# 384-row tiles in four slots, and three engine programs aligned to an instruction block, in a kernel that streams one large input

## The chip, the cores and the metric

The kernel runs on one core of one Trainium2 chip. Its engines are called PE (TensorE), VectorE or DVE, ACT (ScalarE), Pool (GpSimd) and SP (SyncE, which here only issues transfers). The metric is the device time of an execution in microseconds (us), as a median over several executions. Beside it each execution has a *span*, from its first to its last instruction.

## The reference, cut to what matters

```python
B, S, D = 8, 2048, 4096            # x: [B, S, D] float32, w: [D, 1] float32
def reference(x, w):
    proj = (x @ w).squeeze(-1)                      # one dot product for each row of x
    cm = np.maximum.accumulate(proj, axis=1)
    is_record = (proj >= cm).astype(np.float32)
    return np.cumsum(is_record, axis=1).astype(np.float32)
```

x is 268.4 MB and each value is used once; everything after the dot products works on 8 x 2048 numbers.

## The kernel before

The rows are cut into groups: three of 512 rows for each of the 8 batches, one of 384, and 128 last rows that are loaded in small pieces. A tile is one group of one batch. Partition p holds `r` successive rows, so a tile of 512 rows is loaded in 128 runs of 64 KB, one of 384 rows in runs of 48 KB. SP issues all loads of x, in order, on one queue. VectorE takes the first 2816 columns of each row (product and sum in one instruction), Pool multiplies the other 1280, ACT sums them. Pool waits for VectorE's signal `go`, ACT for Pool's products, and SP's next load into a slot for VectorE and ACT.

```python
    RS = (4, 4, 4, 3)                 # rows for each partition in each group
    R = RS[0]; NS = 3                 # three slots of R rows
    NG = len(RS); NL = NG - 1
    ...
        for g in range(NG):
            r = RS[g]
            for t in range(B):
                i = SY.dma_start(
                    out=at(g, t)[:, : r * D],
                    in_=x[B - 1 - t, STARTS[g] : STARTS[g] + r * P, :].rearrange(
                        "(p r) d -> p (r d)", r=r
                    ),
                ).then_inc(xs[t], 16)
                u, n = user_before(g, t)
                if n:
                    i._wait_ge(*(free(u, n)))
                if g == t == 0:
                    A.dma_start(out=w_row, in_=w.rearrange(...)).then_inc(ws, 16)
    ...                               # last 128 rows in pieces; stores of out
        with V.Fori(0, NL):           # the 512-row groups: a loop
            group_scans()
            V.sem_inc(psr, -3)
            group_dots(R)
        group_scans()                 # the 384-row group: once more, unrolled
        V.sem_inc(psr, -3)
        group_dots(RS[-1], NL)
    ...                               # the same loop-and-copy on Pool, ACT and PE
```

Of the kernel before, what the change touches and what calls it, by code (L numbers as in the profile page):

```python
# [20 lines left out]
def kernel(  # L21
# [17 lines left out]
    B, S, D = x.shape  # L39
    WC = 512  # L40
    NW = D // WC
    RS = (4, 4, 4, 3)
    R = RS[0]
    NS = 3
    NG = len(RS)
    NL = NG - 1
    N = R * P
    STARTS = [sum(RS[:g]) * P for g in range(NG)]
    S0 = sum(RS) * P
    assert S0 + P == S  # L50
# [29 lines left out]
    def sb(shape, name, **kw):  # L80
        return pool.tile(shape, FP32, name=name, **kw)
# [5 lines left out]
    w2 = sb([P, W2C], "w2")  # L87
    xall = sb([P, NS * R * D], "xall")
    xbuf = [xall[:, i * R * D : (i + 1) * R * D] for i in range(NS)]
    w_sb = sb([P, PC], "w_sb")  # L90
# [23 lines left out]
    def sem(name):  # L114
        return tc.alloc_semaphore(f"{name}_{next(ns)}")

    xs = [sem("xs") for _ in range(B)]
    fr = [sem("fr") for _ in range(B)]
    xq = [sem("xq") for _ in TILES]
    ws, bw, wc, cs, od, oe, psr, pd, pl, go, sd, pa, con, fo, ms, p7, mg = (  # L120
        sem(n) for n in "ws bw wc cs od oe psr pd pl go sd pa con fo ms p7 mg".split()
    )

    V, A, G, T, SY = nc.vector, nc.scalar, nc.gpsimd, nc.tensor, nc.sync

    def dot(xsl, wsl, dst):
        return V.tensor_tensor_reduce(  # L127
            out=xsl, in0=xsl, in1=wsl, scale=1.0, scalar=0.0,
            op0=ALU.mult, op1=ALU.add, accum_out=dst,
        )  # L130

    def add_up(xsl, dst):
        return A.activation(out=xsl, in_=xsl, func=ACTF.Copy, accum_out=dst)  # L133
# [7 lines left out]
    def scans(cm_, cnt_, src, cm0, cnt0, base=1):  # L141
        low = neg.to_broadcast(list(src.shape))
        V.tensor_tensor_scan(  # L143
            out=cm_, data0=src, data1=low, initial=cm0, op0=ALU.max, op1=ALU.max,
        )._wait_ge(psr, base).then_inc(psr, 1)
        V.tensor_tensor(  # L146
            out=src, in0=src, in1=cm_, op=ALU.is_ge
        )._wait_ge(psr, base + 1).then_inc(psr, 1)
        V.tensor_tensor_scan(  # L149
            out=cnt_, data0=src, data1=low, initial=cnt0, op0=ALU.add, op1=ALU.max,  # L150
        )._wait_ge(psr, base + 2).then_inc(cs, 1)

    def at(g, t):
        return xbuf[(t if g < NL else t + NS - 1) % NS]

    def user_before(g, t):
        if t >= NS:
            return t - NS, g + 1
        if g == NL:
            return B - NS + t, g  # L160
        return max(u for u in range(B) if u % NS == t), g

    def free(u, n):
        return (p7, n) if u == B - 1 else (fr[u], 2 * n)

    with tc.tile_critical(no_gpsimd_drain=True):

        for g in range(NG):
            r = RS[g]
# [11 lines that stand above are left out]
                    A.dma_start(  # L181
                        out=w_row, in_=w.rearrange("(k c) one -> k (c one)", k=NW)
                    ).then_inc(ws, 16)
                if t == 4 and g:
                    SY.dma_start(
                        out=out[:, STARTS[g - 1] : STARTS[g]], in_=cnt
                    )._wait_ge(cs, g + 1).then_inc(od, 16)

        def slot(m):
            if m < NS:  # L190
                return None, xbuf[m][:, RS[-1] * D :]
            u = B - NS if m < 2 * NS else B - NS + 1
            return u, at(NL, u)[:, (m % NS) * D : (m % NS + 1) * D]

        freed = {None}

        for i, (m, c0, c1, _, _) in enumerate(TILES):
            u, xb = slot(m)
            d = SY.dma_start(  # L199
                out=xb[:, c0:c1],  # L200
                in_=x[
                    rows_of(m)[0] : rows_of(m)[0] + H,
                    S0 + rows_of(m)[1] : S0 + rows_of(m)[1] + Q, c0:c1,
                ].rearrange("b i d -> i b d"),
            ).then_inc(xq[i], 16)
            if u not in freed:
                freed.add(u)
                d._wait_ge(*free(u, NG))
            if i == len(TILES) - 4:
                SY.dma_start(  # L210
                    out=out[:, STARTS[-1] : S0], in_=cnt[:, : S0 - STARTS[-1]]
                )._wait_ge(cs, NG + 1).then_inc(oe, 16)
# [42 lines left out]
        def group_scans(r=R):  # L255
            n = r * P
            scans(cm[:, :n], cnt[:, :n], ps[:B, :n], cm[:, N - 1 :], cnt[:, N - 1 :])

        def group_dots(r, g=0):
            for t in range(B):  # L260
                b, xb = B - 1 - t, at(g, t)
                if r == R:
                    V.wait_ge(xs[t], 16).then_inc(go, 1)
                for j in range(r):
                    i = dot(
                        xb[:, j * D : j * D + VC], w_v[:, :VC],
                        sum_v[:, j * B + b : j * B + b + 1],
                    )
                    if j == 0 and r < R:
                        i._wait_ge(xs[t], 16).then_inc(go, 1)  # L270
                    elif j == 1:
                        i.then_inc(xs[t], -16)
                i.then_inc(fr[t], 1)

        with V.Fori(0, NL):
            group_scans()
            V.sem_inc(psr, -3)
            group_dots(R)
        group_scans()
        V.sem_inc(psr, -3)  # L280
        group_dots(RS[-1], NL)

        def group_products(r, g=0):
            for t in range(B):
                for j in range(r):
                    xl = at(g, t)[:, j * D + VC : (j + 1) * D]
                    i = G.tensor_mul(out=xl, in0=xl, in1=w_sb).then_inc(pl, 1)  # L287
                    if j == 0:
                        i._wait_ge(go, 1)
                G.sem_inc(go, -1)  # L290

        G.wait_ge(wc, 3)
        with G.Fori(0, NL):
            group_products(R)
        group_products(RS[-1], NL)

        def group_sums(r, g=0):
            for t in range(B):
                b = B - 1 - t
                for j in range(r):  # L300
                    i = add_up(
                        at(g, t)[:, j * D + VC : (j + 1) * D],
                        sum_p[:, j * B + b : j * B + b + 1],
                    )._wait_ge(pl, j + 1)
                i.then_inc(fr[t], 1)
                A.sem_inc(pl, -r)
            A.wait_ge(pd, 1).then_inc(pd, -1)

        with A.Fori(0, NL):
            group_sums(R)  # L310
        group_sums(RS[-1], NL)

        def group_rows(r):
            T.wait_ge(fr[B - 1], 2).then_inc(p7, 1)
            T.sem_inc(fr[B - 1], -2)
            T.wait_ge(od, 16).then_inc(od, -16)  # L316
            for j in range(r):
                for k, l in enumerate((sum_p, sum_v)):
                    i = T.matmul(  # L319
                        out=ps[:B, j : r * P : r], lhsT=l[:, j * B : (j + 1) * B],  # L320
                        rhs=identity, start=k == 0, stop=k == 1,
                    )
                    if j == r - 1:
                        i.then_inc((pd, psr)[k], 1)

        with T.Fori(0, NL):
            group_rows(R)
        group_rows(RS[-1])


        nv = npool = na = nm = on_a = on_g = 0
# [1 line left out]
        def sums(i, dst_v, dst_p):  # L333
            nonlocal nv, npool, na
            m, _, _, v, p = TILES[i]
            xb = slot(m)[1]
            dot(xb[:, v[0] : v[1]], w_v[:, v[0] : v[1]], dst_v)._wait_ge(
                xq[i], 16
            ).then_inc(sd, 1)
            nv += 1  # L340
            if p:
                xl = xb[:, p[0] : p[1]]
                G.tensor_mul(out=xl, in0=xl, in1=w_pool(*p))._wait_ge(  # L343
                    xq[i], 16
                ).then_inc(pl, 1)
                npool += 1
                add_up(xl, dst_p)._wait_ge(pl, npool).then_inc(pa, 1)
                na += 1
# [90 lines left out]
```

## Time and profile before

| what | value | view |
|---|---|---|
| time, median of 3 (4 with the run beside the changed kernel) | 631.57 (631.58) us | times of the runs |
| span of the profiled execution | 630.02 us | page |
| x queue | 268.50 MB, 98.8% of 16 DMA engines | page, part 3 |
| VectorE busy | 406.9 us (65%) | page, part 1 |
| 512-row tile, landing to landing | 19.35 us (433.5 GB/s) | chain of waits |
| 384-row tile, landing to landing | 14.53 us | chain of waits |
| first x packet starts; last x packet ends | 2.00 us; 624.45 us | packet records of the trace |

The page of the kernel before, its DMA part and one line of the costliest groups (line, engine, operation, operands, count, then busy us and mean ns of one, then idle time before and what ended it):

```profile
DMA  9999999999999999999999999999999999999995
...
DMA packets 6579, 268.55 MB, mean 426 GB/s; under 512 B 768, under 2 KB 1040, under 8 KB 1584
...
q1 hardware_dynamic: 6560, 268.50, 98.8%
...
q14 instruction: 3, 0.02, 0.0%
...
L127 DVE CUSTOM_DVE_ANT_0 xall<-xall,w_v 128x2816 f32<-128x2816 f32 (+3 forms) x133 | 388.4, 2974 | 187.8 <-DMA xall<-in_x_dram 187.8
```

The 16 DMA engines have work in all but the last slice, and VectorE's idle time is all wait for x. The stream is the bound. The line `q14 instruction: 3` is three packets of instructions, of 8,192 bytes each, that were fetched during the span, over the same DMA engines (the one at 126.4 us below starts where an x packet ends, and the next x packet starts where it ends); such a packet is called a fetch or an instruction packet below.

The chain of waits of the kernel before, between 80 and 180 us (start, length, what). A Pool group starts 0.50 to 0.59 us after its 512-row tile has landed (four tiles that land from 80.56 to 139.45 us):

```profile
81.06 11.49 POOL xall L287 x4
...
100.40 11.51 POOL xall L287 x4
111.91 8.05 issue
...
119.99 11.50 POOL xall L287 x4
131.49 8.52 issue
...
140.04 11.50 POOL xall L287 x4
151.55 7.81 issue
...
159.39 0.09 POOL xall L287
```

The starts are 19.34, 19.59, 20.05 and 19.35 us apart. Two tiles came late, by 0.24 and 0.70 us against the usual 19.35, and the stream never got that time back.

Where that comes from stands in the trace's packet records, which give start, length and size of every packet. They don't name the DMA engine, but 99% of the packets of the kernel before start within 0.02 us of the end of an earlier one, so the packets can be strung into 16 chains, taken as the 16 engines. The x queue also has writes of 4 bytes, 16 for each of the 45 loads, of 9 ns each; they are taken as each engine's sign that its part of the load is done, and the last of the 16 gives the landing without any stringing. I use one quantity from this, the **lateness**: how long after the median engine the latest of the 16 finishes its eighth (last) packet of a tile. A tile counts as landed only when its latest engine is done (the seventh tile: median engine 138.21, latest 139.45, Pool starts at 140.04), so here the stream ends with its latest engine. In the kernel before lateness is 0.40 us at the first tile, 1.24 us at the seventh tile and 1.43 us at the last 384-row tile. The step comes with an instruction packet at 126.4 us, which takes 0.33 us on one engine and leaves the next x packet there 0.66 us longer (3.08 us instead of 2.42).

### The profile page before, as it was taken

To read this page: it belongs to the slowest core of one execution; us is meant where nothing else is said; L and a number is where in the kernel's file an instruction comes from. 1 tells how busy PE (TensorE), PEld (TensorE's weight loads), DVE (VectorE), ACT (ScalarE), POOL (GpSimd) and SP (SyncE) were. 2 spreads that over 40 slices of the span, in tenths; PEclk is the share of its full clock that TensorE was granted. 3 is DMA by queue.
4 is the path that set the end of the run, shared out by engine and by line. 5 is a ranking of instruction groups with operands and counts; after the bars stand their busy time and mean duration, and the time that the engine had idled before them with its cause. 6 is when DMAs were issued, how large, how long until landed. Compare 5 with 4: busy or idle time off the path is not lost.

```text
span 630.0 us, 1182 instructions
## 1 busy us (share of the span) xinstructions
PE 31.7 (5%) x108; PEld 15.1 (2%) x108; DVE 406.9 (65%) x292; ACT 180.4 (29%) x273; POOL 370.1 (59%) x147
## 2 busy tenths in 40 slices
PE   8000000000010000000010000000002000000031
PEld 3000000000010000000010000000001000000010
DVE  0755676546785557755579555676557966655897
ACT  1222332123322233222233222332223232232353
POOL 0555676446765557755567555576555766666685
PEclk9999999999999999999996555555555555555555
DMA  9999999999999999999999999999999999999995
GB/s 400 399 466 399 466 408 458 421 442 433 433 441 424 445 424 441 425 445 420 449 416 454 412 458 408 458 408 458 408 425 437 444 418 437 444 415 440 416 424 230
DMA packets 6579, 268.55 MB, mean 426 GB/s; under 512 B 768, under 2 KB 1040, under 8 KB 1584
## 3 DMA queue, kind: packets, MB, share of 16 engines
q1 hardware_dynamic: 6560, 268.50, 98.8%
q10 hardware_dynamic: 16, 0.02, 0.0%
q14 instruction: 3, 0.02, 0.0%
HBM read 268.45 MB, written 0.07 MB: 426 GB/s over the span
## 4 chain that ended last, share of the span: by engine, by line
POOL 52%; issue 38%; DMA 6%; PE 2%; DVE 1%; SPq 0%; POOLq 0%; ACT 0%; ACTq 0%
POOL xall L287 52%; DMA xall<-in_x_dram 6%; PE w_v L231 2%; PE ps L231 0%; DVE xall L127 0%; SPq L199 0%; DMA w<-in_w_dram 0%; POOLq L290 0%; ACT w L242 0%; PE ps L373 0%; DVE cm_l L143 0%; DVE cnt_l L149 0%; DVE ps L146 0%; ACT xall L133 0%; DVE masked L365 0%
## 5 line engine op out<-in xcount | busy, mean ns | idle before, releaser
L127 DVE CUSTOM_DVE_ANT_0 xall<-xall,w_v 128x2816 f32<-128x2816 f32 (+3 forms) x133 | 388.4, 2974 | 187.8 <-DMA xall<-in_x_dram 187.8
L287 POOL TENSOR_TENSOR xall<-xall,w_sb 128x1280 f32<-128x1280 f32 x120 | 344.9, 2909 | 250.2 <-POOLq L290 250.2
L133 ACT ACTIVATE xall<-xall 128x1280 f32<-128x1280 f32 (+1 forms) x130 | 162.8, 1252 | 429.7 <-POOL xall L287 417.1
L319 PE MATMUL ps<-identity,small 128*8 128x128 f32 x60 | 13.1, 410 | 572.0 <-PEq L316 572.0
L133 ACT ACTIVATION_READ_ACCUMULATOR xall<-xall 128x1 f32 x130 | 24.2, 186 | 0.0
L343 POOL TENSOR_TENSOR xall<-xall,w_sb 128x1280 f32<-128x1280 f32 (+1 forms) x8 | 21.6, 2704 | 2.8 <-DMA xall<-in_x_dram 2.8
L319 PEld LDWEIGHTS ps<-identity,small 128*8 128x8 f32 x60 | 7.5, 128 | 578.8 <-issue 574.8
L143 DVE TENSOR_TENSOR_SCAN cm<-ps,cm,small 8x512 f32<-8x512 f32 (+1 forms) x5 | 6.1, 1216 | 14.1 <-PE ps L319 14.1
L231 PE MATMUL w_v<-w,identity 8*128 8x512 f32 x14 | 12.1, 1056 | 0.0
L127 DVE DVE_READ_ACCUMULATOR2_ANT small<- 128x1 f32 x133 | 10.8, 82 | 0.0
L253 DVE MEMSET ps<- 8x512 f32 x1 | 0.5, 485 | 15.5 <-ACT w L242 15.5
L149 DVE TENSOR_TENSOR_SCAN cnt<-ps,cnt,small 8x512 f32<-8x512 f32 (+1 forms) x5 | 6.1, 1217 | 0.2
L373 PE MATMUL ps<-fold,masked 128*8 128x64 f32 x32 | 4.6, 303 | 20.1 <-ACT masked L361 13.2
L231 PEld LDWEIGHTS w_v<-w,identity 8*128 8x128 f32 x14 | 4.6, 332 | 7.3 <-issue 7.3
L239 ACT COPY w_sb<-w_v 128x768 f32<-128x768 f32 x1 | 0.8, 799 | 11.4 <-PE w_v L231 11.4
L146 DVE TENSOR_TENSOR ps<-ps,cm 8x512 f32<-8x512 f32 (+1 forms) x5 | 3.3, 660 | 0.2
L373 PEld LDWEIGHTS ps<-fold,masked 128*8 128x8 f32 x32 | 2.5, 112 | 22.4 <-ACT masked L361 14.6
L361 ACT ACTIVATE masked<-fold,small 128x8 f32<-128x8 f32 x9 | 2.5, 297 | 0.2
L231 PE MATMUL ps<-w,identity 8*128 8x512 f32 x2 | 2.1, 1136 | 2.6 <-DMA w<-in_w_dram 2.6
L238 ACT ACT_TABLE_LOAD x1 | 1.3, 1283 | 2.7 <-DVE fold L249 2.7
L245 DVE TENSOR_REDUCE fold<-identity 128x2 f32<-128x128 f32 x1 | 0.3, 286 | 2.1 <-POOL cnt L224 2.1
L343 POOL TENSOR_TENSOR xall<-xall,w 128x352 f32<-128x352 f32 (+1 forms) x2 | 1.5, 766 | 0.2 <-DMA xall<-in_x_dram 0.2
(23 smaller groups left out, 7.0 us busy)
## 6 DMA issues: line engine op xcount, KB each, us to landing
xall<-in_x_dram SPq DMA_DIRECT2D x8, 6144.0 KB, 30.5
xall<-in_x_dram SPq DMA_DIRECT2D x6, 2048.0 KB, 39.5
xall<-in_x_dram SPq DMA_DIRECT2D x1, 1200.0 KB, 33.5
xall<-in_x_dram SPq DMA_DIRECT2D x1, 848.0 KB, 35.1
xall<-in_x_dram SPq DMA_DIRECT2D x1, 752.0 KB, 36.3
xall<-in_x_dram SPq DMA_DIRECT2D x1, 576.0 KB, 37.1
xall<-in_x_dram SPq DMA_DIRECT2D x24, 45.0
xall<-in_x_dram SPq DMA_DIRECT2D x1, 352.0 KB, 17.4
```

What stands on the lines that cost most here:

```text
L127: return V.tensor_tensor_reduce(out=xsl, in0=xsl, in1=wsl, scale=1.0, scalar=0.0, op0=ALU.mult, op1=ALU.add, accum_out=dst,)
L133: return A.activation(out=xsl, in_=xsl, func=ACTF.Copy, accum_out=dst)
L143: V.tensor_tensor_scan(out=cm_, data0=src, data1=low, initial=cm0, op0=ALU.max, op1=ALU.max,)._wait_ge(psr, base).then_inc(psr, 1)
L146: V.tensor_tensor(out=src, in0=src, in1=cm_, op=ALU.is_ge)._wait_ge(psr, base + 1).then_inc(psr, 1)
L149: V.tensor_tensor_scan(out=cnt_, data0=src, data1=low, initial=cnt0, op0=ALU.add, op1=ALU.max,)._wait_ge(psr, base + 2).then_inc(cs, 1)
L231: i = T.matmul(out=dst, lhsT=identity[:NW, k : k + 1].to_broadcast([NW, P]), rhs=w_row, start=True, stop=True,).then_inc(bw, 1)
L238: A.copy(out=w_sb[:, CV - VC :], in_=ps)._wait_ge(bw, 1).then_inc(wc, 1)
L287: i = G.tensor_mul(out=xl, in0=xl, in1=w_sb).then_inc(pl, 1)
L319: i = T.matmul(out=ps[:B, j : r * P : r], lhsT=l[:, j * B : (j + 1) * B], rhs=identity, start=k == 0, stop=k == 1,)
L343: G.tensor_mul(out=xl, in0=xl, in1=w_pool(*p))._wait_ge(xq[i], 16).then_inc(pl, 1)
L361: A.activation(out=e, in_=on, func=ACTF.Copy, scale=acc)._wait_ge(*wait).then_inc(ms, 1)
L373: return T.matmul(out=ps[:B, q : q + Q], lhsT=e, rhs=by_i, start=start, stop=bool(stop),)._wait_ge(*((mg, on_g) if pool else (ms, on_a)))
```

## The change

It makes all five groups 384 rows, in four slots of three rows (the same bytes), so that each engine has one loop and no unrolled second copy. It also asks, with `addr_align(128, 2)`, that the programs of VectorE, ACT and Pool start at slot 2 of a block of 128 instruction slots; with 109, 75 and 85 instructions they stay below that number. The aim is to keep instruction fetches out of the stream. No trace names the length of a block; what the traces show is where the three instruction packets of the span lie: at 116, 126 and 496 us before.

```diff
-    RS = (4, 4, 4, 3)
+    RS = (3, 3, 3, 3, 3)
     R = RS[0]
-    NS = 3
+    NS = 4
 ...
     with tc.tile_critical(no_gpsimd_drain=True):
+        for eng in (V, A, G):
+            eng.addr_align(128, 2, max_nops=0)
 ...
-                if r == R:
-                    V.wait_ge(xs[t], 16).then_inc(go, 1)
                 for j in range(r):
                     i = dot(...)
-                    if j == 0 and r < R:
+                    if j == 0:
                         i._wait_ge(xs[t], 16).then_inc(go, 1)
 ...
-        with V.Fori(0, NL):
+        with V.Fori(0, NG):
             group_scans()
             V.sem_inc(psr, -3)
             group_dots(R)
-        group_scans()
-        V.sem_inc(psr, -3)
-        group_dots(RS[-1], NL)
```

The same loop-without-copy stands on Pool, ACT and PE; the slot arithmetic becomes `xbuf[t % NS]`. In instructions: VectorE 185 to 109, ACT 116 to 75, Pool 125 to 85, PE 63 to 52.

More of the change, by code (lines that the diff above doesn't have):

```diff
@@ L41 @@
     NW = D // WC
-    RS = (4, 4, 4, 3)
+    RS = (3, 3, 3, 3, 3)
     R = RS[0]
-    NS = 3
+    NS = 4
     NG = len(RS)
-    NL = NG - 1
     N = R * P
@@ L153, in at @@
     def at(g, t):
-        return xbuf[(t if g < NL else t + NS - 1) % NS]
+        return xbuf[t % NS]
     def user_before(g, t):
-        if t >= NS:
-            return t - NS, g + 1
-        if g == NL:
-            return B - NS + t, g
-        return max(u for u in range(B) if u % NS == t), g
+        return (t - NS, g + 1) if t >= NS else (t + B - NS, g)
     def free(u, n):
@@ L189, in slot @@
         def slot(m):
-            if m < NS:
-                return None, xbuf[m][:, RS[-1] * D :]
-            u = B - NS if m < 2 * NS else B - NS + 1
-            return u, at(NL, u)[:, (m % NS) * D : (m % NS + 1) * D]
-        freed = {None}
+            u = B - NS + m // R
+            return u, at(NG, u)[:, m % R * D : (m % R + 1) * D]
+        freed = set()
         for i, (m, c0, c1, _, _) in enumerate(TILES):
@@ L292 @@
         G.wait_ge(wc, 3)
-        with G.Fori(0, NL):
+        with G.Fori(0, NG):
             group_products(R)
-        group_products(RS[-1], NL)
         def group_sums(r, g=0):
@@ L307, in group_sums @@
             A.wait_ge(pd, 1).then_inc(pd, -1)
-        with A.Fori(0, NL):
+        with A.Fori(0, NG):
             group_sums(R)
-        group_sums(RS[-1], NL)
         def group_rows(r):
@@ L324, in group_rows @@
                         i.then_inc((pd, psr)[k], 1)
-        with T.Fori(0, NL):
+        with T.Fori(0, NG):
             group_rows(R)
-        group_rows(RS[-1])
         nv = npool = na = nm = on_a = on_g = 0
```

## The prediction

> **What bounds the kernel.** The stream of x. The page's DMA part gives its queue 268.50 MB and 98.8% of 16 engines' span, at a mean of 426 GB/s. [...] a 512-row tile (8.389 MB) lands every 19.348 us, 433.6 GB/s. VectorE (406.9 us busy) waits for tiles. Of the 630.0 us span, about 2.2 us pass before the first x packet and about 5.3 after the last; neither is touched. In steady state a slot is free about 13 us after its tile landed while two further tiles (38.7 us) are queued: about 26 us of slack.
>
> **What changes, costed.**
> 1. 24 tiles of 512 rows and 8 of 384 become 40 of 384. A 64 KB packet takes 2.419 us of its engine (packet records), a 48 KB one 1.818: 17 ns of fixed cost per packet. By landings, 384-row tiles come every 14.530 us, so 1536 rows cost 58.121 us instead of 58.044. Over the 24 replaced tiles: **+0.6 us**, all critical.
> 2. Four slots of 3 rows hold the same bytes as three of 4. Slack becomes 3 x 14.53 - 13.2, about 30 us. Worth **0**. Pool starts each tile with VectorE's first dot finished, 3.15 us late (the last group's timeline shows this already): also 0.
> 3. Instruction fetches. The trace has three 8 KB packets of the instruction queue inside the span, at 116.5, 126.6 and 496.6 us. Each takes 0.31 to 0.33 us on one of the 16 DMA engines, and the x packet beside it takes 0.35 to 0.66 us longer. One engine loses 0.98 us at 126.6 and never gets it back: a tile's last engine finishes 0.42 us after the median one at tiles 0 to 4, and 1.24 to 1.37 us after it from tile 6 to the end. The stream ends with that straggler. From slot 2 of a 128-slot block, VectorE's program (about 107 slots), ACT's and Pool's each fit one block, and no fetch should fall into the stream. Saved: about 0.98 less what the next-latest engine costs, **-0.8 us**. [...]
> 4. The alignment adds a jump to VectorE, ACT and Pool at the start, perhaps a fetch, before x's packets. The first tile lands at about 17 us, its first dot starts at about 21 to 24; the slack absorbs it: **0**.
> 5. The tail (last group, single-row tiles, last pieces) keeps its sizes: **0**.
>
> **Sum.** 631.57 + 0.6 - 0.8 = **631.3 us**, range **630.6 to 632.2**. Faster by over 2%: 0.01; within 2%: 0.98; slower: 0.01.
>
> **What would show it.** Step 1: 48 KB packets at 1.82 us and landings every 14.53 us throughout. Step 3: no instruction packet between about 3 and 625 us, and a last-to-median spread that stays near 0.4 us. Step 2: DMA still 98 to 99%. Step 4: the first VectorE dot waits for the scans, not for DMA. Step 5: 5 to 5.5 us from last packet to end.
>
> **What would make it wrong.** A fetch caused by the alignment that falls on the first x packets would put the straggler back (about +0.8). 48 KB packets slower in the early groups than in the last one. A late engine that the fetches did not cause.

Two passages are cut from the text, because no trace or run shows what they said; no term of the sum went with them, so +0.6 and -0.8 and the 631.3 us stand. That a program inside one block brings no fetch into the stream was an expectation when it was written; the changed kernel's trace has since shown no instruction packet from 5.04 us to the end. The 17 ns for a packet is an estimate from the 64 KB and 48 KB packets of the kernel before (2.42 and 1.82 us); e4 below gives 9.5 ns.

## More of the kernel before

Executions of one kernel differ by some tenths of a microsecond: the spans of the kernel before, 50 executions beside the experiments, lie between 629.6 and 630.5 us with a median of 629.9.

## The result, and the profile after

The changed kernel takes **632.62 us** (632.54 to 632.80, 4 executions) against 631.58 us (631.42 to 631.84) of the kernel before beside it: 1.04 us slower, ratio 1.0016 with a 95% interval of 0.9999 to 1.0034. A ratio is the mean time of one kernel's runs over that of the other's of the same rounds, so it is not quite the ratio of the medians. A second set (e10 below) gave 632.59 against 631.66 us. That is within 2%, as forecast, but outside the stated range of 630.6 to 632.2.

The page of the changed kernel, DMA part, VectorE's dots and, in the last line, the 384-row loads (count, KB each, median us from issue to landing):

```profile
span 630.5 us, 1214 instructions
...
DMA packets 7747, 268.55 MB, mean 426 GB/s; under 512 B 904, under 2 KB 1208, under 8 KB 1728
...
q1 hardware_dynamic: 7728, 268.50, 98.9%
q14 instruction: 3, 0.02, 0.0%
...
L126 DVE CUSTOM_DVE_ANT_0 xall<-xall,w_v 128x2816 f32<-128x2816 f32 (+3 forms) x133 | 388.9, 2973 | 164.1 <-DMA xall<-in_x_dram 164.1
...
xall<-in_x_dram SPq DMA_DIRECT2D x40, 6144.0 KB, 44.9
```

VectorE still waits for x alone, and there are still three instruction packets. The chain of waits shows that they are no longer in mid-stream (same stretch as above):

```profile
80.23 8.61 POOL xall L277 x3
...
94.75 8.61 POOL xall L277 x3
...
109.29 8.61 POOL xall L277 x3
...
123.82 0.09 POOL xall L277
```

Starts 14.52, 14.54 and 14.53 us apart: no late tile. So the intended effect is there, and yet the span is 0.46 us longer (630.48 against 630.02). The start shows where the packets went. First the kernel before, then the changed one (timeline: start, length, engine, line, operation; `SPq` and `ACTq` are the issuing queues; `PEld` waits for w):

```profile
0.92 0.61 ACTq L181 DMA_DIRECT2D w<-in_w_dram  x1
...
0.97 35.30 SPq L171 DMA_DIRECT2D xall<-in_x_dram  x4
...
2.62 0.49 PEld L231 LDWEIGHTS ps<-w,identity 8*128 8x128 f32 x2 [2.62 <-DMA w<-in_w_dram]
...
23.07 3.09 DVE L127 CUSTOM_DVE_ANT_0 xall<-xall,w_v 128x2816 f32<-128x2816 f32 x1 [1.10 <-DMA xall<-in_x_dram]
```

```profile
0.96 2.79 SPq L168 DMA_DIRECT2D xall<-in_x_dram  x4
1.36 3.05 ACTq L178 DMA_DIRECT2D w<-in_w_dram  x1
...
11.62 0.50 PEld L226 LDWEIGHTS ps<-w,identity 8*128 8x128 f32 x2 [11.62 <-DMA w<-in_w_dram]
...
30.11 3.05 DVE L126 CUSTOM_DVE_ANT_0 xall<-xall,w_v 128x2816 f32<-128x2816 f32 x1
```

The jump costs ACT 0.44 us before it can issue the load of w, which now stands behind four loads of x and lands at 11.6 us. The three instruction packets are at 1.97, 1.98 and 4.73 us (1.14, 0.91 and 0.31 us long), among the first x packets, which start at 2.0 us. And the lateness is already 1.00 us at the first tile.

The ends of the two executions (last load's first dot, then the last store):

```profile
623.09 0.99 DVE L127 CUSTOM_DVE_ANT_0 xall<-xall,w_v 128x800 f32<-128x800 f32 x1 [0.26 <-DMA xall<-in_x_dram]
...
627.48 0.31 SPq L407 DMA_DIRECT2D out_dram<-cnt_l  x1
```

```profile
623.53 0.99 DVE L126 CUSTOM_DVE_ANT_0 xall<-xall,w_v 128x800 f32<-128x800 f32 x1 [0.21 <-DMA xall<-in_x_dram]
...
627.94 0.31 SPq L394 DMA_DIRECT2D out_dram<-cnt_l  x1
```

Both are shifted by the same amount, 0.44 and 0.46 us, so the tail is unchanged. From the last x packet to the end of the span it is 5.57 us before and 5.56 us after.

One thing is not in the span at all. In the kernel before, time minus span is 1.74 to 1.85 us in 50 executions, mean 1.78. In the changed kernel it is 2.04 to 2.10 in the first four. Some 0.28 us of the 1.04 lie outside the span.

### The profile page after: what moved, and what is told of

It reads as the page before. It is cut to its first block, busy times and chain, and to the rows that moved or that the text cites. A ratio compares the mean times of both kernels' runs of the same rounds, so it can differ in the third digit from the quotient of the medians.

```text
span 630.5 us, 1214 instructions
## 1 busy us (share of the span) xinstructions
PE 32.2 (5%) x108; PEld 14.9 (2%) x108; DVE 407.0 (65%) x295; ACT 180.3 (29%) x273; POOL 369.7 (59%) x147
## 3 DMA queue, kind: packets, MB, share of 16 engines
q1 hardware_dynamic: 7728, 268.50, 98.9%
## 4 chain that ended last, share of the span: by engine, by line
POOL 51%; issue 37%; DMA 7%; PE 2%; DVE 1%; SPq 0%; POOLq 0%; ACT 0%; ACTq 0%
POOL xall L277 51%; DMA xall<-in_x_dram 6%; PE w_v L226 2%; DMA w<-in_w_dram 2%; DVE xall L126 0%; PE ps L226 0%; SPq L194 0%; POOLq L280 0%; ACT w L237 0%; PE ps L360 0%; DVE cm_l L142 0%; DVE cnt_l L148 0%; DVE ps L145 0%; ACT xall L132 0%; POOLq L283 0%
## 5 line engine op out<-in xcount | busy, mean ns | idle before, releaser
L142 DVE TENSOR_TENSOR_SCAN cm<-ps,cm,small 8x384 f32<-8x384 f32 x6 | 6.0, 1003 | 29.1 <-PE ps L307 29.1
L148 DVE TENSOR_TENSOR_SCAN cnt<-ps,cnt,small 8x384 f32<-8x384 f32 x6 | 6.0, 1004 | 0.2
L145 DVE TENSOR_TENSOR ps<-ps,cm 8x384 f32<-8x384 f32 x6 | 3.3, 554 | 0.2
L226 PE MATMUL ps<-w,identity 8*128 8x512 f32 x2 | 2.1, 1136 | 11.6 <-DMA w<-in_w_dram 11.6
```

The source lines that it names most:

```text
L142: V.tensor_tensor_scan(out=cm_, data0=src, data1=low, initial=cm0, op0=ALU.max, op1=ALU.max,)._wait_ge(psr, base).then_inc(psr, 1)
L145: V.tensor_tensor(out=src, in0=src, in1=cm_, op=ALU.is_ge)._wait_ge(psr, base + 1).then_inc(psr, 1)
L148: V.tensor_tensor_scan(out=cnt_, data0=src, data1=low, initial=cnt0, op0=ALU.add, op1=ALU.max,)._wait_ge(psr, base + 2).then_inc(cs, 1)
L226: i = T.matmul(out=dst, lhsT=identity[:NW, k : k + 1].to_broadcast([NW, P]), rhs=w_row, start=True, stop=True,).then_inc(bw, 1)
```

## The experiments

Each run was timed beside the kernel before on the same chip. All passed the comparison with the reference (e14 to e16 load some wrong rows; the comparison did not flag it). This table, worked out from the times and packet records, gathers them:

```
run                    time   before*  span**  time-   lateness (us) at          last x    instruction packets
                       (us)   (us)     (us)    span    1st tile  last 384-row   ends (us)  after 1.5 us, at (us)
before                631.58    -      629.9   1.78    0.40      1.43            624.45    116, 126, 496
after                 632.62  631.58   630.55  2.07    1.00      1.05            624.92    1.97, 1.98, 4.73
e10 after, again      632.59  631.66   630.5   2.06    1.01      1.23            625.22    1.99, 2.28, 5.00
e1  no align          632.47  631.70   630.4   2.06    0.87      0.99            624.93    123, 590, 593
e11 no align, again   632.86  631.66   630.8   2.08    1.13      1.07            625.30    123, 590, 593
e2  before + align    632.67  631.70   630.9   1.78    0.88      2.10            625.27    1.98, 2.13, 5.33, 532, 573
e3  early align       632.18  631.70   630.1   2.04    0.61      0.62            624.49    1.77, 1.82, 1.95
e4  one-row loads     638.42  631.70   636.6   1.80    0.87      0.99            631.01    1.97, 1.99, 4.04, 330
e5  before + 9 on SP  632.01  631.94   629.9   2.09    0.45      0.97            624.74    117, 127, 497
e6  after + 24 on SP  632.55  631.94   630.8   1.79    0.93      1.21            625.20    1.96, 1.97, 4.77, 589
e7  before, early     632.00  631.94   630.2   1.79    0.23      1.28            624.44    1.75, 1.79, 1.94, 531, 573
e8  w first           632.47  631.94   630.4   2.06    0.78      0.82            624.59    1.97, 4.53, 6.48
e9  early + 24 on SP  632.65  631.66   630.9   1.77    0.76      0.63            625.30    1.78, 1.86, 1.94, 589
e12 three loads first 632.62  631.63   630.55  2.07    0.92      1.00            624.89    123, 590, 593
e13 before, first 48K 631.55  631.63   629.75  1.81    0.31      1.10            624.21    116, 126, 497
e14 e13, 48 KB apart  631.82  631.70   630.05  1.79    1.33      1.20            624.48    119, 126, 497
e15 no align, 64 apart632.24  631.70   630.15  2.09    0.32      0.91            624.56    123, 590, 593
e16 e15 + early align 631.74  631.67   629.7   2.05    0.21      0.39            624.18    1.76, 1.82, 1.92
*  median of the kernel before in the same rounds   ** median of the run's executions; lateness and
   what stands right of it are from the one profiled execution; the row "before" has the median of the 50 spans
```

The instruction packets at 589 to 593 us come after the last 384-row tile. By the 4-byte writes, lateness at the fifth one-row tile (at about 609 us) is 1.08 in e1, 1.38 in e11, 0.74 in e12 (where the median engine moved back), 0.93 in e15, 1.43 in e6 and 1.35 in e9; in the other runs it is as in the table.

### e1 to e3: which part of the change costs

e1 takes the alignment away, e2 gives it to the kernel before, e3 places it earlier, ahead of the barrier that starts the engines.

```diff
# e1 (from after)                      # e2 (from before): the same two lines added
-        for eng in (V, A, G):
-            eng.addr_align(128, 2, max_nops=0)
# e3 (from e1)
+    for eng in (nc.vector, nc.scalar, nc.gpsimd):
+        eng.addr_align(128, 2, max_nops=0)
     with _tile.TileContext(nc) as tc:
```

> The changed kernel without the alignment of the three programs. Theory A (two parts: 48 KB packets cost about 0.6 us over the stream, and the alignment moves three instruction fetches from mid-stream onto the first x packets, where they make one engine about 1.0 us late and put the load of w behind four x loads): w is back before 3 us, the last-to-median spread of the first tile is about 0.4 us, instruction packets come back at about 100 to 130 us, and the spread goes to about 1.2 us after them. Span about 630.6 us, time about 632.2. If the alignment costs nothing at all (rival B: all of the loss is the 384-row tiles) the time stays at 632.6.

> The kernel before with the alignment alone. Theory A: two instruction packets near 2 us on top of the first x packets, spread of the first tile about 1.0 us instead of 0.4, w lands after 8 us instead of before 3, no instruction packets at 116 and 126 us, but VectorE's program (185 slots and more) still crosses into a second block, in the last 384-row group at about 480 us. Time 631.6 to 632.1. Rival B: 631.6, as before.

> The changed kernel with the three alignments moved ahead of the barrier between the engines at the start, so that the jump is taken earlier. Theory A: the instruction packets come some 0.4 to 0.8 us earlier and partly miss the first x packets; the last-to-median spread of tile 0 falls from 1.0 towards 0.4 us, w is back before 3 us, and the time is 632.0 to 632.4. Rival B: 632.6.

e1 is 0.77 us above the kernel before of its rounds, the repeat e11 1.20. So taking the alignment away does not give the time back. Two expectations failed. The first tile's lateness was not 0.4 but 0.87, with no instruction packet near: the start of the 384-row stream is uneven by itself. And time minus span stayed 2.06.

e2 was slower than the kernel before by 0.97 us, more than either theory had allowed. The chain of waits of e2 shows the step (in the kernel before Pool starts a 384-row tile 3.66 us after its landing, at 512.21, 526.75, 555.90 and 570.43 us alike, so the starts are as far apart as the landings):

```profile
530.26 8.61 POOL xall L289 x3
...
545.77 8.62 POOL xall L289 x3
...
560.39 8.62 POOL xall L289 x3
...
574.92 8.62 POOL xall L289 x3
```

15.51 us instead of 14.53, then 14.62 and 14.53. The instruction packet at 532 us hit the engine that was the latest already; lateness went from 1.08 to 2.10. In the kernel before three instruction packets hit three engines, two of which had time to lose: lateness went from 0.42 to 0.55 us with the packet at 116 us, and stayed at 1.36 to 1.37 with the one at 496 us. They take 0.31, 0.33 and 0.31 us, and the next x packet there is 0.38, 0.66 and 0.35 us longer than the usual 2.42 or 1.82 us: 0.69, 0.98 and 0.66 us in all. Whether that costs the kernel anything depends, in these traces, on the engine it hits. The two packets that e2 keeps in mid-stream came at 532 and 573 us, where one at about 480 us was expected; the records do not name the engine that fetched.

In e3 two of the fetches come some 0.2 us earlier and the third 2.8 us earlier, so that all three start before the first x packet does at 2.02 us (the third lasts until 2.80). Lateness is 0.61 at the start and 0.62 at the end, the span 0.45 us shorter than the changed kernel's. That is what theory A forecast, but its reason is not shown: e1 and its repeat e11, which have no fetch at the start at all, start later (0.87 and 1.13) than e3. Why the early jump helps stays open.

### e4: the packets themselves

```diff
-                i = SY.dma_start(
-                    out=at(g, t)[:, : r * D],
-                    in_=x[...].rearrange("(p r) d -> p (r d)", r=r),
-                ).then_inc(xs[t], 16)
+                for j in range(r):
+                    i = SY.dma_start(
+                        out=at(g, t)[:, j * D : (j + 1) * D],
+                        in_=x[...].rearrange("(p r) d -> p r d", r=r)[:, j, :],
+                    ).then_inc(xs[t], 16)
 ...
-                        i._wait_ge(xs[t], 16).then_inc(go, 1)
+                        i._wait_ge(xs[t], 16 * r).then_inc(go, 1)
```

> The changed kernel with each 384-row tile loaded by three DMAs of one row for each partition: same bytes, same slots, 16 KB packets instead of 48 KB. Theory A: a packet costs a fixed 15 to 17 ns beside its bytes, so that three rows on an engine go from 1.816 to 1.836 us (from the landings of the 16 KB and 48 KB loads in the profile before); 320 such triples on each engine cost 6.2 us: 638.8 us. Rival C: what costs is the number of DMAs and their completion counts, 9 ns for each on every engine: 80 more cost 0.7 us, 633.3 us.

638.42 us, 5.8 above the changed kernel; the last x packet ends 6.08 us later. The page of e4:

```profile
span 636.6 us, 1294 instructions
...
DMA packets 19268, 268.56 MB, mean 422 GB/s; under 512 B 2184, under 2 KB 2488, under 8 KB 3008
...
q1 hardware_dynamic: 19248, 268.51, 99.3%
```

The bytes are the same and the engines as busy, only the packets are smaller. Rival C (0.7 us, from the 9 ns that a 4-byte write takes in the trace before) is ruled out as the whole. Each of the 16 DMA engines moves 640 packets more than in the changed kernel, so one more packet costs 9.5 ns (6.08 us / 640), the writes of the additional loads included. That is less than the "15 to 17 ns" of the expectation, whose own sum, 20 ns for two more packets, comes to 10. So 48 KB instead of 64 KB has a price. In the two profiled executions, from the first tile to the last whole one-row tile the median engine of the changed kernel needs 0.62 us more than that of the kernel before, after the different length of the first tile (19.35 against 14.53 us) is taken off.

### e5 and e6: the part outside the span

Time minus span is 1.8 us for SP programs of 68 or 157 instructions and 2.05 for 77. e5 and e6 add instructions on SP at a point where it waits for a slot.

```diff
+                if g == 1 and t == 2:          # e6: g == 2, and 24 of them
+                    for _ in range(9):
+                        SY.sem_inc(pad, 1)     # a semaphore that nothing waits for
                 if t == 4 and g:
```

> The kernel before with 9 more instructions on the SP queue (increments of an unused semaphore, at a point where SP waits for a slot), so that SP's program is 77 instructions long as in the changed kernel, instead of 68. The time of a run stands 1.77 us above its span in the kernel before, in e2 (SP 68) and e4 (SP 157), and 2.05 us above it in the changed kernel, e1 and e3 (SP 77). Theory D: the 0.28 us are set by where SP's program ends in an instruction block: span as before (about 629.9), time minus span 2.05, time 631.9. Rival E: they belong to the 384-row tiles (the last store, or the sums): time minus span stays 1.77, time 631.6.

> The changed kernel with 24 more instructions on the SP queue, put where SP waits, so that its program (101) ends well inside the next block. Theory D: time minus span goes back to 1.77; one more instruction packet (SP's own) falls into the stream, which costs nothing unless it hits the latest engine; time 632.3 to 632.5. Rival E: time minus span stays 2.05, time 632.6 or more.

Theory D held both ways. The kernel before with 77 instructions on SP has 2.03 to 2.12 us between time and span, its median span unchanged (the profiled execution is its slowest, 632.42 us: all engines lost some 0.7 us before 120 us). The changed kernel with 101 has 1.75 to 1.81. So 0.28 us come from the length of SP's program, and the 384-row tiles have to do with it only because they need nine more instructions. Why a length of 77 costs it is not shown. Theory D's reason, where the program ends in an instruction block, fits the packets (e4's SP program of 157 has one at 330 us, e6's of 101 one at 589 us, the changed kernel's of 77 none in mid-stream), but no record reaches behind the span.

In time e6 is 632.55 us, 0.61 above the kernel before of its rounds, where the changed kernel was 1.04 and 0.93 above. e5 is 0.07 above. The rounds of e5 to e8 need care: the kernel before itself stood 0.3 us higher in them (631.94 us, span 630.2) than in the others, so a difference of that size between sets proves nothing. The difference of time and span, which has a scatter of 0.1 us at most, is what the verdict rests on.

### e7: the alignment ahead of the barrier in the kernel before

> The kernel before (64 KB packets) with the alignment ahead of the barrier, as in e3. Theory A with one addition, that the end of the stream is the end of its latest engine: the latest engine starts about 0.6 us after the median (e3) instead of 1.0 (e2); the instruction packets at about 532 and 573 us of e2 stay, [...] and each adds 0.7 to 1.0 us to one engine. If they hit engines that are not late: latest engine 1.1 us after the median, 631.2 us, the fastest so far. If one hits the latest again, as in e2 (2.1): 632.2.

e7 is the kernel before with the two lines of e3. It takes 632.00 us against 631.94 of the kernel before: no gain. The start is the most even so far (0.23), and then the packet at 531 us puts 0.97 us on one engine (lateness 0.33 to 1.28). With the unrolled copies (185, 116 and 125 instructions) two packets in mid-stream are left (531 and 573 us), and one of them is enough to hold the end. The clause cut from the expectation said whose packets they are, which no record shows. The hope for 631.2 fell.

### e8: the late w

```diff
                     A.dma_start(out=w_row, in_=w.rearrange(...)).then_inc(ws, 16)
+                    for eng in (V, A, G):
+                        eng.addr_align(128, 2, max_nops=0)
```

(and the same two lines taken out at the top)

> The changed kernel with ACT's alignment after its load of w, so that the load is issued ahead of the four x loads. Theory A: w lands before 3 us instead of after 11, the first dot starts at about 21 us instead of 30, and the time does not change (632.4 to 632.7), since the slots' slack of some 30 us holds both. Rival F: the late w is what costs: 631.8 or less.

The timeline of e8:

```profile
0.92 0.60 ACTq L176 DMA_DIRECT2D w<-in_w_dram  x1
0.96 2.60 SPq L166 DMA_DIRECT2D xall<-in_x_dram  x4
...
3.51 0.50 PEld L226 LDWEIGHTS ps<-w,identity 8*128 8x128 f32 x2 [3.51 <-DMA w<-in_w_dram]
...
21.99 3.05 DVE L126 CUSTOM_DVE_ANT_0 xall<-xall,w_v 128x2816 f32<-128x2816 f32 x1
```

w is back 8 us and the first dot starts 8 us earlier than in the changed kernel, for a time of 632.47 (631.94 beside it) and a span of 630.4 us instead of 630.5. Rival F is ruled out: the slots' slack holds a late w. The lateness of the profiled execution was 0.8.

### e9 to e11: both cures, and repeats

> The changed kernel with both cures: the alignment ahead of the barrier (e3) and 24 more SP instructions (e6). If the two costs are separate and add, time minus span is 1.78 instead of 2.05 and the latest engine ends about 0.4 us earlier in the span: 631.9 to 632.1, level with the kernel before, with the 0.6 us of the 48 KB packets left. If they are one cost seen twice, 632.2, as e3.

> The changed kernel unchanged, on the same chip as e9 and e11, for a second trace of its start: if the alignment's fetches make the late engine, tile 0's last engine is again 0.8 to 1.1 us after the median; span 630.4 to 630.7, time minus span 2.05, 632.5 to 632.7.

> The changed kernel without the alignment once more (e1), for a second trace: in e1 one engine began 1 us late with no instruction packet near, and tile 0's last engine was 0.87 us after the median. If that was chance of one execution, it is now 0.4 to 0.6 us, as in the two traces with 64 KB packets and no alignment (0.40 and 0.45); if the 48 KB loads do it, 0.8 to 0.9 again. Span 630.2 to 630.5, 632.3 to 632.5.

e9 is e3 and e6 together. The part outside the span was 1.77 as expected, but the time was 632.65 us, 0.6 above what was expected, and the span 630.9 instead of 630.1. The trace shows why. At the last 384-row tile lateness is 0.63, as in e3. Then comes SP's own instruction packet at 588.8 us, which the 24 added instructions bring, and it hits one of the latest engines: it takes 0.31 us there, the next x packet takes 1.03 us instead of 0.61, and lateness is 1.35 from then on. Pool's start on the fifth one-row tile is 0.80 us later in e9 (second line) than in e3 (first line):

```profile
610.07 2.90 POOL L328 TENSOR_TENSOR xall<-xall,w_sb 128x1280 f32<-128x1280 f32 x1 [0.59 <-DMA xall<-in_x_dram]
```

```profile
610.87 2.90 POOL L332 TENSOR_TENSOR xall<-xall,w_sb 128x1280 f32<-128x1280 f32 x1 [0.92 <-DMA xall<-in_x_dram]
```

So each cure did what it did alone, but the second brought a fetch that cost 0.7 us here (0.2 in e6), and the two do not add up in time. e10 confirms the changed kernel: 1.01 us late at the first tile, 632.59 us. e11 confirms that the uneven start needs no alignment: 1.13.

Together with e12 below, these runs test step 3 of the prediction alone, with the same loads. The spans are 630.4, 630.8 and 630.55 us with the fetches in mid-stream (e1, e11, e12) and 630.55 and 630.5 us without (after, e10): no gain. The packet at 123 us leaves lateness nearly as it was (0.87 at the first and 0.99 at the last 384-row tile in e1, 1.13 and 1.07 in e11, 0.92 and 1.00 in e12), since an engine that was late from the start stays the latest.

### e12 to e15: why the start of the 384-row stream is uneven

The traces up to here can be sorted by how late the latest engine ends its first x packet: 0.29 to 0.45 us after the median with 64 KB loads (before, e2, e5, e7), 0.67 to 1.21 us with 48 KB loads (after, e1, e3, e6, e8 to e11), with or without alignment. The first loads of the two kernels differ in how many are issued at once, in the packet size, and in where the runs lie in memory. e12 holds the fourth load back until w has landed; e13 cuts the first load of the kernel before in a 48 KB and a 16 KB part.

```diff
# e12 (from e1)
+                if g == 0 and t == 3:
+                    i._wait_ge(ws, 16)
# e13 (from before), first load only
+                    xr = x[B - 1, : r * P, :].rearrange("(p r) d -> p r d", r=r)     # r = 4
+                    SY.dma_start(out=at(g, t)[:, : 3 * D]..., in_=xr[:, :3, :]).then_inc(pad, 16)
+                    i = SY.dma_start(out=at(g, t)[:, 3 * D :], in_=xr[:, 3, :]).then_inc(xs[t], 16)
 ...
+        V.wait_ge(pad, 16)
```

> The changed kernel without the alignment (e1, e11), with the fourth load of x held back until w has landed, so that three loads are issued at once at the start, as in the kernel before. In the traces so far the first x packet of the latest engine ends 0.29 to 0.45 us after the median one with 64 KB loads (4 traces, with and without alignment) and 0.67 to 1.21 us after it with 48 KB loads (8 traces). Theory G: the number of loads issued at once makes it: now 0.3 to 0.5 us. Theory H: the size of the first packets makes it: 0.7 to 1.2 us as before. Time about 632.0 under G, 632.5 under H.

> The kernel before, where only the first load is cut in two: 48 KB packets (three rows) and 16 KB packets (one row); everything after is 64 KB. Theory H: the first packet of the latest engine ends 0.7 to 1.2 us late, and the tile's last engine with it. Theory G (four loads at once, as here, instead of three): the same; together with e12 they separate: e12 late and e13 late is H, e12 even and e13 late is G, e12 late and e13 even leaves both wrong. Time 631.6 to 632.0, for what follows is as before.

e12 was late (0.92), e13 even (0.31): neither the number of loads nor the packet size. What is left is the distance. In the kernel before, the runs of successive partitions start 64 KB apart in memory, in e13 too, where the fourth row is left out. In the changed kernel they start 48 KB apart. e14 and e15 exchange just that, for the first load alone.

```diff
# e14 (from e13): 384 rows that follow one another, 48 KB apart
-   in_=xr[:, :3, :]                        -   in_=xr[:, 3, :]
+   in_=x[B - 1, : 3 * P, :].rearrange("(p r) d -> p (r d)", r=3)
+   in_=x[B - 1, 3 * P : 4 * P, :]          # second part
# e15 (from e1): three of every four rows, 64 KB apart
-   in_=x[B - 1, : 3 * P, :].rearrange("(p r) d -> p (r d)", r=3)
+   in_=x[B - 1, : 4 * P, :].rearrange("(p r) d -> p r d", r=4)[:, :3, :]
```

> As e13, but the three-row part of the first load takes 384 rows that follow one another (48 KB from one partition's run to the next, as in the changed kernel) instead of three of every four rows (64 KB apart), and the one-row part the 128 rows after them. The rows are then in a wrong order and the result is wrong on purpose. Theory I: the distance of the runs in memory, 48 KB instead of 64 KB, makes the uneven start: first packet of the latest engine 0.7 to 1.2 us late. If not: 0.3 to 0.45, as e13.

> The changed kernel without the alignment, where the first load takes three of every four rows of the first 512 (runs of 48 KB that lie 64 KB apart, as in e13); wrong rows, so wrong on purpose. Theory I: the start is even, 0.3 to 0.45 us for the first packet of the latest engine, and the stream ends some 0.5 us earlier than in e1 and e11 (span about 630.1, time about 632.1). If not: 0.87 to 1.2 us, span 630.4 to 630.8.

```
first x packet of each DMA engine, us     starts: median  last    ends: median  last    last - median
e13  before, 48 KB runs 64 KB apart               2.15    2.66          4.67    4.98    0.31
e14  before, 48 KB runs 48 KB apart               2.17    3.42          4.76    6.19    1.43
e11  changed, no alignment, 48 KB apart           2.34    3.48          4.91    6.07    1.16
e15  changed, no alignment, 64 KB apart           2.30    3.07          4.75    5.07    0.32
```

Both came out as theory I expects. The first packets of the kernel before become uneven (1.43) when its first load takes runs 48 KB apart, and those of the 384-row stream become even (0.32) when they lie 64 KB apart. The distance of the runs of the first load is shown to be the cause, in both directions; it is one trace each, on the same chip, and e16 below repeats the even start. What goes with the distance, such as whether every run starts at a multiple of 64 KB, was not separated from it. Later tiles keep the lateness but do not add to it (e11: 1.13 at the first tile, 1.07 at the last 384-row tile), so as far as these traces show, the distance matters only while the stream starts. What in the memory makes it so, no run here shows. Nor does an uneven start simply add to the fetches: e14 starts 1.33 and ends 1.20 us late, e13 starts 0.31 and ends 1.10, for the end is that of one engine, whichever is the latest.

e15 ends with a lateness of 0.9, which rises from 0.32 to 0.66 with the fetch at 123 us and in small steps after it; its span is 630.15 against 630.4 and 630.8 of e1 and e11.

### e16: even start and no fetch in mid-stream

e16 is e15 with the alignment ahead of the barrier.

> The changed kernel with the alignment ahead of the barrier (e3) and the first load's runs 64 KB apart (e15; one tile's rows wrong on purpose): an even start and no instruction packet in mid-stream, which is what the prediction had taken for granted. If lateness adds up as the runs so far say, the latest engine is 0.25 to 0.4 us after the median from the first tile to the last, the stream ends near 624.0, the span is 629.5 to 629.8, and the time, with SP's program still at 77 instructions (2.06 above the span), 631.5 to 631.9. If something else holds the end, the span stays 630.1.

The span is 629.7 us (629.8 in the profiled execution), 0.45 below e15's and 0.8 below the changed kernel's, and lateness is 0.21 at the first tile and 0.39 at the last 384-row tile. The time is 631.74 us: level with the kernel before (631.67), with the 0.6 us of smaller packets and the 0.28 us of SP's length still in it. This kernel loads one tile's rows wrongly, so it is a measurement and not a version to use. A version that beats both kernels beyond the noise was not found.

## Why the prediction was wrong

The prediction was +0.6 for packets and -0.8 for fetches, 631.3 us in sum. Measured is 632.62. The two profiled executions (631.80 and 632.54 us) can be taken apart, by the fifth one-row tile at about 608 us: the median engine is 0.87 us later (608.00 to 608.87), the latest engine's lead over it 0.39 us smaller (1.44 to 1.05), the tail the same, and the part outside the span about 0.27 us longer. That makes 0.75 us, and the two times differ by 0.74. The other 0.3 us of the medians' 1.04 is where these two executions lie among their own kind: the one of before 0.22 above its median, the one of after 0.08 below.

1. **Bound.** Right. The stream bounds both kernels, DMA at 98.8 and 98.9%, with a 512-row tile in 19.35 us, 433.5 GB/s.
2. **Step 1, +0.6 us for smaller packets.** Right in kind and size: 0.62 us by the median engine, landings 14.52 to 14.54 us, and e4 with 16 KB packets adds 6.1 us to the stream where 6.2 was expected. The other 0.25 of the 0.87 is at the first tile, where traces of one kind scatter by 0.3 and where a start with runs 48 KB apart also puts the median engine later (22.41 us in e14, 22.21 in e13; 17.53 and 17.62 in e1 and e11, 17.43 in e15).
3. **Step 2, slots, 0.** Right. DMA stayed at 98.9%, and e8 shows that 8 us more or less at the first dot move nothing.
4. **Step 3, -0.8 us for the fetches. This is the step that failed.** "No fetch should fall into the stream" was right for mid-stream: no packet between 5.1 us and the end. The mistake was the next half, "a last-to-median spread that stays near 0.4 us". The 0.4 was read from the start of the kernel before and carried over to a kernel with a different first load. The 384-row stream starts 0.9 to 1.1 us uneven by itself (e1, e11, e12), because its runs lie 48 KB apart (e14, e15). One engine is then late from the first tile on, with or without fetches in mid-stream, and taking these out gained nothing (spans 630.55 and 630.5 us against 630.4, 630.8 and 630.55). That is the last risk the prediction itself named, "a late engine that the fetches did not cause". With an even start the step holds: the 629.7 us of e16 fit the 629.9 of the kernel before with 0.6 added and 0.8 taken off. The size of the gain was also read from one trace, where the fetch happened to leave one engine 1.43 us late; e5, with the same three programs, ends with 0.97.
5. **A term that was missing, +0.28 us.** Eight loads and one store more on SP lengthen its program to 77 instructions, and the time outside the span from 1.78 to 2.06 us (e5, e6). The prediction costed the span only.
6. **Step 4, the jump, 0.** Right for w, with a larger delay than thought: w lands at 11.6 us and the first dot starts at 30.1 instead of 21 to 24, yet the slack holds it (e8). The first risk that the prediction named, that a fetch of the alignment on the first x packets puts the late engine back, is not shown for the changed kernel: the fetches did fall there, but the first tile's lateness is 0.78 to 1.01 us with them (after, e6, e8, e10) and 0.87 to 1.13 without (e1, e11, e12). In the kernel before, one trace has 0.88 with them and 0.40 without (e2).
7. **Step 5, the tail, 0.** Right: 5.57 and 5.56 us. The text's "2.2 us before the first packet and 5.3 after the last" put the start of the span 0.23 us too early; it is 2.0 and 5.57, and the packets of the kernel before are at 116.3, 126.4 and 496.4 us. Nothing rested on it.

## What to carry to other kernels

In this saturated stream (98.8 and 98.9% of 16 engines' span) the end was the end of its latest DMA engine, and what one engine lost early was hardly ever won back (lateness 1.24 us at the seventh tile and 1.43 at the last 384-row tile before, 1.00 at the first and 1.05 at the last 384-row tile after). In such a stream look at the latest engine and not only at the mean rate, and ask of each cause whether it hits the engine that is already late. Before the removal of a disturbance is costed, ask what else makes one engine late: here a different first load made one late from the start (first x packet 1.43 us after the median in e14, 0.32 in e15), and the removal alone was worth nothing (spans 630.55 and 630.5 us against 630.4 to 630.8). Take "it was even before" from a kernel with the same first load, and from several executions; and compare time with span, because the cost of something as small as nine instructions on an issuing engine lay outside the span here (1.78 to 2.09 us in e5).
